# The attention of a decoder's second layer, moved from 49 single units to 33 steps of one or two, with its products in another order

## The chip, the cores and the metric

The kernel runs on one core of a Trainium2 chip. The metric is the device time of one execution in microseconds (us), taken as the median of several runs. The engines are named as in the profile: PE (TensorE, matrix products and transposes), PEld (its weight loads), DVE (VectorE), ACT (ScalarE), POOL (GpSimd) and SP (the queue that issues most DMAs).

## The reference

One inference step of a two-layer decoder for a prompt of 512 positions and 8 samples of 4 new positions each. Layer 1 is a Mamba-2 mixer; then one shared K/V is computed; layer 2 is attention in three dilation groups over that K/V, which the change is about. All arithmetic is in f32.

```python
D_MODEL, SEQ, DEC_BATCH, DEC_SEQ, PAST_LEN = 1024, 512, 8, 4, 1024
ATT_HEAD_DIM = 128; KV_HEADS = 8
WINDOWS, DILATIONS = (128, 512, 2048), (1, 4, 16)

def dilated_attn_prompt(q, k, v, bvec, dil, nw):      # and the same for samples, over the cached K/V
    scores = jnp.einsum("brnqhd,brnkhd->brnhqk", qs, kb) * (dh ** -0.5)
    scores = jnp.where(valid[None, None], scores + bias, NEG_INF)
    lse = jax.nn.logsumexp(scores, axis=-1)
    p = jnp.exp(scores - lse[..., None])
    o = jnp.einsum("brnhqk,brnkhd->brnqhd", p, vb)
    ...
def dilated_mixer(h, attend, biases, g_norm, w_in, w_out):
    u = rmsnorm(h, g_norm) @ w_in
    q, gate = ...                                     # 3 x 8 heads of queries, and a gate per head
    for g in range(N_DIL_GROUPS):
        o, lse = attend(q[:, :, g], biases[g], DILATIONS[g], WINDOWS[g] // DILATIONS[g])
    w = jax.nn.softmax(jnp.stack(lses, axis=0), axis=0)
    o = jnp.sum(w[..., None] * jnp.stack(outs, axis=0), axis=0)
    y = o.reshape(b, l, ATT_WIDTH) * jax.nn.silu(gate)
    return y.astype(h.dtype) @ w_out
```

## The kernel before, in words

The program is written in Python; a scheduler sets each engine's order from it, close to the order of writing. Each engine then works through its own queue in order and waits at an instruction whose inputs or buffers are not ready. Blocks marked `tc.high_priority()` are put earlier.

Layer 2 interleaves two streams on PE. The first is the *filler*: the projections of queries and gate, in products of 12 matmuls each (`product`, three for each of four blocks of the inner dimension, 128x272 results, tiles `pa` and `pb`). One filler matmul is called F. Seven products make a pair of heads' tiles, from sums and differences of weights (`sums`, L1266 to L1272). `cast(b + 3)` splits the weights of the product three ahead in a high part `whi` (ACT, L1289) and a low part `wlo` (DVE, L1290), into one of four buffers, which product b - 1 frees with its last matmul. Evacuations of the products are L1218 to L1244 (`qp`, `kv`, `us`, `y`; `u2`, `u3` appear as sums) and L1327 to L1333. `run(n)` issues the next n F. After the projections the filler goes on with the out projection, which needs the gated `y` split in high and low part (`yh` L1345, `yl` L1346).

The second stream is the attention, in *units*, each a generator that stops at `yield`:

- `attend(h, n)`, 32 times: head h, 128 queries of the prompt. Scores `sp` are one full product and eight (for the dilated groups) on 32 of the array's columns, "tiled" below; then on DVE two reduces (L1392, L1395) and the maximum (L1397), on ACT the exponential (L1398), on DVE an add of two groups and a reciprocal (L1399, L1400). Stop. Transposes `ptp` of the weights, copied on ACT to `pt`, `ptz`. Stop. The products with the values, `pv`, full ones and then tiled ones; `on` on ACT (L1419). Stop. Transpose `op`; a head's fourth goes to `y`.
- `sample(h, q)`, 16 times: four samples of head h. Cached keys `kc` come by DMA; scores `s` are tiled; softmax on DVE and ACT (L1460 to L1465). Stop. Transposes `w`. Stop. Products `so` with cached values, all tiled.
- `combine`, once: weights of the groups for all samples. Ln, `lse` (L1492), transpose `lp`, a softmax over groups (L1498 to L1516). Stop. Transpose `lp2`. Stop. Products `oc`.

The order is set by the list `units` and the loop at the end of the layer: pass u lets three older units go on by one stop (u - 4, then u - 2, then u - 3), starts unit u, and issues 24 F (20 from unit 44 on). `LA = 2` is the distance from a unit's start to its second part.

Of the kernel before, what the change touches and what calls it, by code (L numbers as in the profile page):

```python
# [34 lines left out]
ATH = 8  # L35
# [19 lines left out]
OCN, SKIP = 2, 1  # L55
POOL_A = (0, 1, 2, 3)
POOL_B = (0, 1, 2)
PRO, OFF, PACE = 9, 8, (57, 62, 64, 44)
LA, FILL, SLOW = 2, (24, 20), 44
TH = T // 2  # L60


# [65 lines left out]
def tile_yoco_step(  # L128
# [16 lines left out]
    def mm(*a, **k):  # L145
        pin(nc.tensor.matmul(*a, **k))  # L146
# [767 lines left out]
    live = []  # L914
# [457 lines left out]
    def attend(h, n):  # L1372
        bt, qp = bt_t[h], [qp_t[h, g] for g in range(3)]
        kv = kv_t[h]
        kt = kv[:, 0, :]
        vb, vr = (kv[:, i, 0:SEQ].rearrange("p (n d) -> p n d", n=4) for i in (1, 2))
        kp = kt[:, NS:T]
        ktr = kp.rearrange("p (n r i) -> p r n i", n=4, r=4)
        bt12 = bt[:, 256:512].rearrange("p (a c) -> p a c", a=2)
        w = 32 * (n + 1)  # L1380
        g0 = 128 if n == 0 else 256
        sp = pss("sp")
        k0 = max(0, n - 1) * 128
        for g in range(2):
            for r in range(4):
                mm(sp[32 * r:32 * r + 32, g0 + w * g:g0 + w * g + w],
                   qp[1 + g][:, 128 * n + 32 * r:128 * n + 32 * r + 32], ktr[:, r, 0:n + 1, :], start=True, stop=True)
        mm(sp[:, 0:g0], qp[0][:, 128 * n:128 * n + 128], kp[:, k0:128 * n + 128], start=True, stop=True)
        s_ = wk.tile([128, 512], F32, name="s", bufs=3)
        mx = wk.tile([128, 4], F32, name="mx", bufs=4)  # L1390
        s12 = s_[:, g0:g0 + 2 * w].rearrange("p (a c) -> p a c", a=2)
        nc.vector.tensor_tensor_reduce(out=s12, in0=sp[:, g0:g0 + 2 * w].rearrange("p (a c) -> p a c", a=2),  # L1392
                                       in1=bt12[:, :, 128 - w:128], scale=1.0, scalar=-3e38,
                                       op0=ALU.add, op1=ALU.max, accum_out=mx[:, 1:2])
        nc.vector.tensor_tensor_reduce(out=s_[:, 0:g0], in0=sp[:, 0:g0], in1=bt[:, 256 - g0:256], scale=1.0,  # L1395
                                       scalar=-3e38, op0=ALU.add, op1=ALU.max, accum_out=mx[:, 0:1])
        nc.vector.tensor_scalar(mx[:, 2:3], mx[:, 0:1], mx[:, 1:2], -1.0, op0=ALU.max, op1=ALU.mult)  # L1397
        nc.scalar.activation(s_[:, 0:g0 + 2 * w], s_[:, 0:g0 + 2 * w], AF.Exp, bias=mx[:, 2:3], accum_out=mx[:, 3:4])  # L1398
        nc.vector.tensor_tensor(s12[:, 0, :], s12[:, 0, :], s12[:, 1, :], op=ALU.add)  # L1399
        nc.vector.reciprocal(mx[:, 3:4], mx[:, 3:4])  # L1400
        yield
        tp = pss("ptp", (128, 3, 128))
        nk = g0 // 128
        for i in range(nk):
            transpose(tp[:, i, :], s_[:, 128 * i:128 * i + 128], ident)
        transpose(tp[0:w, 2, :], s_[:, g0:g0 + w], ident)
        pt = wk.tile([128, 2, 128], F32, name="pt", bufs=2)
        nc.scalar.copy(pt[:, 0:nk, :], tp[:, 0:nk, :])
        nc.scalar.copy(ptz[n][0:w, :], tp[0:w, 2, :])
        yield  # L1410
        pv = pss("pv")[:, 0:128]
        for i in range(nk):
            b = n - nk + 1 + i
            mm(pv, pt[:, i, :], vb[:, b, :], start=i == 0, stop=False, skip_group_check=True)
        for r in range(4):
            mm(pv[32 * r:32 * r + 32, :], ptz[n][:, 32 * r:32 * r + 32], vr[:, r, :],
               start=False, stop=True, skip_group_check=True)
        on = wk.tile([128, 128], F32, name="on", bufs=1)
        nc.scalar.activation(on, pv, AF.Copy, scale=mx[:, 3:4])  # L1419
        yield  # L1420
        if h not in op_t:
            op_t[h] = pss("op")
        op = op_t[h]
        transpose(op[:, 128 * n:128 * n + 128], on, ident)
        op_n[h] = op_n.get(h, 0) + 1
        yt = y_t[h // 4][:, h % 4, :]
        if h == 7 and op_n[h] >= 3:
            c0, c1 = ((128, SEQ), (0, 128))[op_n[h] - 3]
            y7 = yt[:, NS + c0:NS + c1]
            assert len(gated) == 2  # L1430
            nc.vector.scalar_tensor_tensor(y7, op[:, c0:c1], 0.5, y7, op0=ALU.mult, op1=ALU.mult)
            y_split(h, NS + c0, NS + c1)
        elif h < 7 and op_n[h] == 4:
            nc.vector.tensor_copy(yt[:, NS:T], op)
            att_done.add(h)
# [5 lines left out]
    def sample(h, q):  # L1441
# [27 lines left out]
        for jp in range(2):  # L1469
            vc.append(wk.tile([128, 2, 5, 128], F32, name="vc", bufs=2))  # L1470
            dma(vc[jp], cv[h, q, :, 2 * jp:2 * jp + 2, :, :])
        yield
        dma(vn[0:TS], dap(vnd, h * 128 + 4 * q * TS * ATH * 128, [[ATH * 128, TS], [TS * ATH * 128, 4], [1, 128]]))
        w1, w2 = pss("w1", (128, 4, 128)), pss("w2", (128, 2, 128))
        for i in range(5):
# [2 lines left out]
        nc.scalar.copy(wt[:, 0:4, :], w1)  # L1478
        nc.scalar.copy(wt[:, 4, :], w2[:, 0, :])
        nc.scalar.copy(wt[0:TS, 5, :], w2[0:TS, 1, :])  # L1480
        yield
        so = pss("so")[:, 0:128]
        for i in range(6):
# [6 lines left out]
    def combine():  # L1490
        nc.scalar.activation(lsm, lsm, AF.Ln)
        nc.vector.tensor_tensor(lse, lsm, lse, op=ALU.subtract)  # L1492
        lp = pss("lp")
        transpose(lp[0:16, 0:128], lse, ident)
        ltr = qpad[0][0:16]
        lt = ltr[:, 0:4, :]
        with tc.high_priority():
            nc.vector.tensor_copy(lt.rearrange("p a b -> p (a b)"), lp[0:16, 0:128])  # L1498
        lv = lt[:, :, 0:12].rearrange("p j (g t) -> p j t g", t=TS)
        lgv = lt[:, :, 0:12].rearrange("p j (g t) -> p g j t", t=TS)  # L1500
        red = ltr[:, 4, :].rearrange("p (a j t) -> p a j t", a=2, t=TS)
        mxg, sm_ = red[:, 0], red[:, 1]

        def all_groups(a):
            return a[:, None, :, :].to_broadcast([16, 3, 4, TS])

        with tc.high_priority():
            nc.vector.tensor_reduce(out=mxg, in_=lv, axis=AX.X, op=ALU.max)
            for g in range(3):
                nc.vector.tensor_tensor(lgv[:, g], lgv[:, g], mxg, op=ALU.subtract)  # L1510
            nc.scalar.activation(lt[:, :, 0:12], lt[:, :, 0:12], AF.Exp)
            nc.vector.tensor_reduce(out=sm_, in_=lv, axis=AX.X, op=ALU.add)
            nc.vector.reciprocal(sm_, sm_)
            for g in range(3):
                nc.vector.tensor_tensor(lgv[:, g], lgv[:, g], sm_, op=ALU.mult)
            nc.vector.memset(lt[:, :, 12:32], 0.0)  # L1516
        yield
        lp2 = pss("lp2")
        transpose(lp2[:, 0:16], lt.rearrange("p a b -> p (a b)"), ident[0:16, 0:16])
        cmw = sbt[:, 0:272].rearrange("p (a b) -> p a b", b=16)  # L1520
        ws, cm = cmw[:, 16, :], cmw[:, 0:16, :]
        with tc.high_priority():
            nc.vector.tensor_copy(ws, lp2[:, 0:16])
            nc.vector.tensor_tensor(cm, sel[:, None, :].to_broadcast([128, 16, 16]), bc(ws, 16), op=ALU.mult)
        yield
        oc = pss("oc", (128, ATH, 2, 16))
        for h in range(ATH):
            for q in range(2):
                mm(oc[:, h, q, :], o_s[:, q, h, :], cm[:, 2 * h + q, :], start=True, stop=True)
                if q:  # L1530
                    run(OCN)
        nc.scalar.copy(y_s, oc.rearrange("p h q c -> p h (q c)"))
        sample_y()
# [102 lines left out]
    def run(n):  # L1636
        m = min(n, ahead[0]) if n > OCN else 0
        ahead[0] -= m
        for _ in range(n - m):
            if next(fill, 0) == 0:  # L1640
                return

    units = [(f, (h, i)) for h in range(ATH - 1) for f, i in
             ((attend, 0), (sample, 0), (attend, 1), (attend, 2), (sample, 1), (attend, 3))]
    units += [(sample, (7, 0)), (attend, (7, 1)), (attend, (7, 2)), (sample, (7, 1)), (attend, (7, 3)), (combine, ()), (attend, (7, 0))]
    fill = filler()
    fetch_kv(0)
    for _ in range(2 * 84):
        next(fill)
    fetch_kv(1)  # L1650
    live = []
    for u in range(len(units) + LA + 2):
        i = u - LA
        if u == len(units) - 2 + SKIP:
            ahead[0] = ATH * OCN
        for j in (i - 2, i, i - 1):
            if 0 <= j < len(units):
                next(live[j], 0)
        if u < len(units):
            f, a = units[u]  # L1660
            if f is attend and a[0] not in bt_t:
                bt_t[a[0]] = bias_tile(a[0])
            if f is attend and a[1] == 2 and 0 < a[0] < ATH - 1:
                fetch_kv(a[0] + 1)
            live.append(f(*a))
            next(live[u])
        run(FILL[u >= SLOW])
    run(10000)
    bctx.close()

# [94 lines left out]
```

## Time and profile before

| | |
|---|---|
| Runs | 928.69, 927.66, 925.65 us; median 927.66 |
| Profiled execution | 932.11 us, its span 930.2 us |
| Granted clock of PE, mean | 0.996 |
| Busy over the span | PE 908.9, PEld 847.9, DVE 687.5, ACT 489.9, POOL 163.0 us |
| Attention stretch, 593.30 to 875.00 us | PE busy for 279.24 of 281.70 us |

The profiled execution is longer than the median of the runs. Rows of the profile name an engine, the line of the helper or program that issued the instruction, and the tiles: all matrix products stand under L146 and all transposes under L149, so they are told apart by tile (`sp`, `s`, `pv`, `so` and so on), with the pair `128*128` or `128*32` for a full or a tiled product. A bracket at a row's end is the time that the engine had been idle, and what released it.

### The profile page before, as it was taken

The page shows a single profiled execution, that of the slowest core. Times are in us where ns is not written, and L with a number is a line of the kernel's source. Part 1 is how long each engine was busy: PE and PEld are TensorE (multiplying, and loading weights), DVE is VectorE, ACT ScalarE, POOL GpSimd, SP SyncE. Part 2 cuts the span into 40 slices and gives each one's busy share as a digit, 9 for nine tenths or more (in the row PEclk, how much of TensorE's full clock was granted, in tenths as well). Part 3 has the DMA queues.
Part 4 walks back from the last instruction along what each step waited for, and adds up shares of the span by engine and source line. Part 5 has one row for each costly group of instructions (what it writes and reads, how often), then busy time and mean ns, then how long its engine had stood idle before and what let it go on. Part 6 is the DMA issues. An engine that isn't in the chain of part 4 may idle for free.

```text
span 930.2 us, 21888 instructions
## 1 busy us (share of the span) xinstructions
PE 908.9 (98%) x8671; PEld 847.9 (91%) x8671; DVE 687.5 (74%) x1435; ACT 489.9 (53%) x1140; POOL 163.0 (18%) x212
## 2 busy tenths in 40 slices
PE   8999999999999999999999999999999999999997
PEld 7989888888989889999999999999899999989997
DVE  6998899989799899644489335876677766778732
ACT  6678655655566655422255213555455555557642
POOL 2031344433514642111101001000000000000021
PEclk9999999999999999999999999999999999999999
DMA  8224365355364442536277556757768868774511
GB/s 295 93 74 155 104 206 166 121 170 170 134 201 161 149 165 101 156 108 228 90 256 227 183 184 196 265 182 264 252 203 262 280 204 267 270 256 155 194 49 49
DMA packets 80573, 168.48 MB, mean 181 GB/s; under 512 B 19990, under 2 KB 37736, under 8 KB 79960
## 3 DMA queue, kind: packets, MB, share of 16 engines
q1 hardware_dynamic: 73784, 154.60, 50.5%
q10 hardware_dynamic: 5616, 9.75, 2.8%
q0 software_dynamic: 1072, 2.74, 1.1%
q8 instruction: 68, 1.11, 0.5%
q14 instruction: 33, 0.27, 0.1%
HBM read 141.14 MB, written 25.93 MB: 180 GB/s over the span
## 4 chain that ended last, share of the span: by engine, by line
PE 82%; DVE 9%; DMA 4%; ACT 2%; issue 2%; POOL 0%; SPq 0%; POOLq 0%; DVEq 0%; ACTq 0%
PE pa L146 33%; PE pb L146 28%; PE sp L146 3%; PE pv L146 2%; PE so L146 2%; PE s L146 2%; DVE wlo L206 2%; DMA kc<-ck 1%; PE yd L146 1%; DMA m<-aed 1%; DVE co L641 1%; PE csp L146 1%; PE w L149 1%; PE ptp L149 1%; PE xp L149 1%
## 5 line engine op out<-in xcount | busy, mean ns | idle before, releaser
L205 ACT ACTIVATE whi<-wraw 128x1024 fp32r<-128x1024 f32 x69 | 72.8, 1056 | 97.0 <-PE pb L146 57.2
L206 DVE TENSOR_TENSOR wlo<-wraw,whi 128x1024 fp32r<-128x1024 f32 x69 | 89.6, 1298 | 45.1 <-ACT whi L205 44.7
L146 PE MATMUL pa<-bq,whi 128*128 128x272 f32 x512 | 103.1, 296 | 0.0
L146 PE MATMUL pb<-nl,whi 128*128 128x288 f32 x280 | 84.0, 300 | 0.0
L146 PE MATMUL pb<-nh,wlo 128*128 128x288 f32 x280 | 83.5, 298 | 0.0
L146 PE MATMUL pb<-nh,whi 128*128 128x288 f32 x280 | 83.4, 298 | 0.0
L146 PEld LDWEIGHTS pa<-bq,whi 128*128 128x128 f32 x512 | 81.2, 189 | 0.9
L146 PE MATMUL pa<-nh,whi 128*128 128x256 f32 x280 | 81.1, 290 | 0.5 <-DVE uz L681 0.5
L146 PE MATMUL pa<-nl,whi 128*128 128x256 f32 x280 | 80.7, 288 | 0.0
L146 PE MATMUL pa<-nh,wlo 128*128 128x256 f32 x280 | 80.1, 286 | 0.0
L146 PE MATMUL pb<-bq,whi 128*128 128x272 f32 x384 | 77.2, 296 | 1.3 <-DVE kv L1230 1.1
L146 PE MATMUL pa<-bq,wlo 128*128 128x272 f32 x256 | 74.2, 290 | 0.0
L641 DVE SCALAR_TENSOR_TENSOR co<-cb,cvp,co 128x568 f32<-128x568 f32 x72 | 64.0, 892 | 1.5 <-ACT co L639 0.9
L146 PEld LDWEIGHTS pb<-bq,whi 128*128 128x128 f32 x384 | 60.8, 189 | 2.6 <-DVE kv L1230 1.3
L1289 ACT ACTIVATE whi<-wraw 128x512 fp32r<-128x512 f32 x64 | 40.1, 627 | 35.2 <-PE pb L146 16.8
L146 PEld LDWEIGHTS pb<-nl,whi 128*128 128x128 f32 x280 | 53.0, 189 | 4.4 <-issue 4.4
L146 PEld LDWEIGHTS pa<-nh,whi 128*128 128x128 f32 x280 | 53.8, 192 | 2.6 <-issue 1.9
L146 PE MATMUL pb<-bq,wlo 128*128 128x272 f32 x192 | 55.5, 289 | 0.0
L146 PEld LDWEIGHTS pa<-nl,whi 128*128 128x128 f32 x280 | 53.8, 192 | 1.4 <-issue 1.4
L146 PEld LDWEIGHTS pb<-nh,wlo 128*128 128x128 f32 x280 | 53.1, 190 | 2.2 <-issue 2.2
L146 PEld LDWEIGHTS pa<-nh,wlo 128*128 128x128 f32 x280 | 53.8, 192 | 0.9 <-issue 0.9
L146 PEld LDWEIGHTS pb<-nh,whi 128*128 128x128 f32 x280 | 53.0, 189 | 0.8 <-issue 0.8
(408 smaller groups left out, 2788.0 us busy)
## 6 DMA issues: line engine op xcount, KB each, us to landing
wraw<-w_in SPq DMA_DIRECT2D x40, 512.0 KB
kc<-ck SPq DMA_DIRECT2D x32, 640.0 KB
vc<-cv SPq DMA_DIRECT2D x32, 640.0 KB
wraw<-wb SPq DMA_DIRECT2D x32, 512.0 KB
s<-s SPq DMA_DIRECT2D x32, 256.0 KB
m<-aed SPq DMA_DIRECT2D x16, 512.0 KB
ssmS<-s ACTq DMA_DIRECT2D x32, 256.0 KB
wraw<-w_out SPq DMA_DIRECT2D x16, 512.0 KB
```

The costliest lines, as they stand in the source:

```text
L146: pin(nc.tensor.matmul(*a, **k))
L149: pin(nc.tensor.transpose(*a))
L205: a = nc.scalar.activation(hi, raw, AF.Copy)
L206: b = lo_eng.tensor_tensor(lo, raw, f32(hi), op=ALU.subtract)
L641: nc.vector.scalar_tensor_tensor(o, cb[:, k:k + n], cvp[:, ti, k:k + 1], o, op0=ALU.mult, op1=ALU.add)
L1289: nc.scalar.activation(hi, src[p][j], AF.Copy)
```

## The change

Units are joined in 33 steps: for each head, sample 0 with block 0, block 1, sample 1 with block 2, block 3 (the last head has its block 0 after `combine`). `LA` is 1: a unit's transposes come one step after its scores. In a pass, the step three back goes on first, then the one before, then the one two back, twice; within a step the prompt's unit goes ahead of the sample's. New stops cut `sp` (tiled | full) and `pv` (full | tiled) so that tiled products of several units follow on each other. Each pass issues 36 F, the last three scored steps 40, 24 and 40, and 20 after that. The lines of the program behind `attend`'s scores move by one to six.

```diff
-LA, FILL, SLOW = 2, (24, 20), 44
+LA = 1
...
                    qp[1 + g][:, 128 * n + 32 * r:128 * n + 32 * r + 32], ktr[:, r, 0:n + 1, :], start=True, stop=True)
+        yield
         mm(sp[:, 0:g0], qp[0][:, 128 * n:128 * n + 128], kp[:, k0:128 * n + 128], start=True, stop=True)
...
             mm(pv, pt[:, i, :], vb[:, b, :], start=i == 0, stop=False, skip_group_check=True)
+        yield
         for r in range(4):
...
-    units = [(f, (h, i)) for h in range(ATH - 1) for f, i in
-             ((attend, 0), (sample, 0), (attend, 1), (attend, 2), (sample, 1), (attend, 3))]
-    units += [(sample, (7, 0)), (attend, (7, 1)), (attend, (7, 2)), (sample, (7, 1)), (attend, (7, 3)), (combine, ()), (attend, (7, 0))]
+    steps = [[(f, (h, i)) for f, i in st] for h in range(ATH - 1) for st in
+             (((sample, 0), (attend, 0)), ((attend, 1),), ((sample, 1), (attend, 2)), ((attend, 3),))]
+    steps += [[(sample, (7, 0)), (attend, (7, 1))], [(attend, (7, 2))], [(sample, (7, 1)), (attend, (7, 3))],
+              [(combine, ())], [(attend, (7, 0))]]
+    fills = [36] * (4 * (ATH - 1)) + [40, 24, 40]
...
-        for j in (i - 2, i, i - 1):
-            if 0 <= j < len(units):
-                next(live[j], 0)
+        for j in (u - LA - 2, u - LA, u - LA - 1, u - LA - 1):
+            if 0 <= j < len(steps):
+                for g_ in live[j][::-1]:
+                    next(g_, 0)
...
+            live.append([f(*a) for f, a in steps[u]])
+            for _ in range(2):
+                for g_ in live[u]:
+                    next(g_, 0)
-        run(FILL[u >= SLOW])
+        run(fills[u] if u < len(fills) else 20)
```

(`sample` has a second `yield` at each of its two stops, and `combine` at its two, to go with the passes.)

The order shows at three places what this moves. Names are as above; `bq` is the filler's input.

**PE, where head 0's block 1 is transposed.** Before:

```order
L149 MATMUL op<-ident,on 128x128
L149 MATMUL ptp<-ident,s 128x128 x2
L149 MATMUL ptp<-ident,s 64x128
L146 MATMUL so<-vc,wt 32x128 x20
L146 MATMUL so<-vn,wt 32x128 x4
L146 MATMUL s_7624<-kc,qpad_7031 32x512 x4
L146 MATMUL s_7625<-kc,qpad_7031 32x128 x4
L146 MATMUL s_7625<-kv,qpad_7031 32x4 x4
L146 MATMUL pb<-bq_6915,whi 128x272 x2
```

And now:

```order
L149 MATMUL ptp<-ident,s 128x128 x2
L149 MATMUL ptp<-ident,s 64x128
L146 MATMUL pv<-kv,pt 128x128
L146 MATMUL pv<-kv,ptz_7035 32x128 x4
L146 MATMUL so<-vc,wt 32x128 x20
L146 MATMUL so<-vn,wt 32x128 x4
L146 MATMUL s_7569<-kc,qpad_7031 32x512 x4
L146 MATMUL s_7570<-kc,qpad_7031 32x128 x4
L146 MATMUL s_7570<-kv,qpad_7031 32x4 x4
L146 MATMUL sp<-kv,qp 32x96 x8
L146 MATMUL sp<-kv,qp 128x256
```

The samples' tiled products stood between a transpose and F in a block of their own; they now lie between the tiled part of `pv` and that of `sp`.

**DVE, around the maximum and the add of head 6's block 2** (`ISA` rows are the reduces; the number behind waits only says for which engine's semaphore). Before:

```order
L1392 ISA s,mx<-sp,bt 128x192 [waits PE_49]
L1392 ISA mx 128x1
L1395 ISA s,mx<-sp,bt 128x256
L1395 ISA mx 128x1
L1397 TENSOR_SCALAR mx<-mx 128x1 [waits DVE_49]
L1329 SCALAR_TENSOR_TENSOR sums<-pb,sums 128x272 [waits PE_49,Activation_49]
L1399 TENSOR_TENSOR s<-s 128x96 [waits Activation_49]
```

And now:

```order
L1290 TENSOR_TENSOR wlo<-sums,whi 128x512 [waits PE_49,Activation_49]
L1237 SCALAR_TENSOR_TENSOR kv<-kv,pa 128x240 [waits Activation_49]
L1272 TENSOR_TENSOR sums<-wraw,sums 128x512 [waits DVE_49]
L1333 SCALAR_TENSOR_TENSOR sums<-pa,sums 128x272 [waits PE_49]
L1290 TENSOR_TENSOR wlo<-wraw,whi 128x512 [waits Activation_49]
L1239 SCALAR_TENSOR_TENSOR us<-kv,pa 128x32
L1244 SCALAR_TENSOR_TENSOR y_7023<-y_7023,kv 128x240 [waits DVE_49]
L1398 TENSOR_SCALAR mx<-mx 128x1
L1400 TENSOR_TENSOR s<-s 128x96 [waits Activation_49]
```

The maximum followed on the reduces; now two casts and the evacuations of two products stand between.

**PE, in the tail, from combine's second transpose on** (`lp_11373` and `lp_11321` are the tile `lp2`). Before, with the transposes of block 3 well ahead of it:

```order
L149 MATMUL op<-ident,on 128x128
L149 MATMUL ptp<-ident,s 128x128 x3
L146 MATMUL so<-vc,wt 32x128 x20
L146 MATMUL so<-vn,wt 32x128 x4
L146 MATMUL sp<-kv,qp 32x32 x8
L146 MATMUL sp<-kv,qp 128x128
L146 MATMUL pa<-bq_6917,wlo 128x272
L146 MATMUL pa<-bq_6917,whi 128x272 x2
L146 MATMUL pa<-bq_6917,wlo 128x272
L149 MATMUL lp_11373<-ident,qpad_7031 128x16
L146 MATMUL pv<-kv,pt 128x128 x2
L146 MATMUL pv<-kv,ptz_7038 32x128 x4
```

And now:

```order
L149 MATMUL lp_11321<-ident,qpad_7031 128x16
L146 MATMUL pv<-kv,pt 128x128 x2
L146 MATMUL pv<-kv,ptz_7038 32x128 x4
L146 MATMUL so<-vc,wt 32x128 x20
L146 MATMUL so<-vn,wt 32x128 x4
L146 MATMUL sp<-kv,qp 32x32 x8
L146 MATMUL sp<-kv,qp 128x128
L146 MATMUL pa<-bq_6917,whi 128x272
L146 MATMUL pa<-bq_6917,wlo 128x272
L146 MATMUL pa<-bq_6917,whi 128x272 x2
L149 MATMUL op<-ident,on 128x128
L149 MATMUL ptp<-ident,s 128x128
```

`lp2` comes ahead of the last samples' products, and the last unit's transposes come after four F and an `op`, where 24 F stood before.

More of the change, by code (lines that the diff above doesn't have):

```diff
@@ L1472, in sample @@
         yield
+        yield
         dma(vn[0:TS], dap(vnd, h * 128 + 4 * q * TS * ATH * 128, [[ATH * 128, TS], [TS * ATH * 128, 4], [1, 128]]))
@@ L1480, in sample @@
         nc.scalar.copy(wt[0:TS, 5, :], w2[0:TS, 1, :])
+        yield
         yield
@@ L1517, in combine @@
         yield
+        yield
         lp2 = pss("lp2")
@@ L1524, in combine @@
             nc.vector.tensor_tensor(cm, sel[:, None, :].to_broadcast([128, 16, 16]), bc(ws, 16), op=ALU.mult)
+        yield
         yield
@@ L1651, in tile_yoco_step @@
     live = []
-    for u in range(len(units) + LA + 2):
-        i = u - LA
-        if u == len(units) - 2 + SKIP:
+    for u in range(len(steps) + LA + 2):
+        if u == len(steps) - 2 + SKIP:
             ahead[0] = ATH * OCN
-        for j in (i - 2, i, i - 1):
-            if 0 <= j < len(units):
-                next(live[j], 0)
[L1659 to L1666, printed above, removed]
-        run(FILL[u >= SLOW])
+        for j in (u - LA - 2, u - LA, u - LA - 1, u - LA - 1):
+            if 0 <= j < len(steps):
+                for g_ in live[j][::-1]:
+                    next(g_, 0)
+        if u < len(steps):
+            for f, a in steps[u]:
+                if f is attend and a[0] not in bt_t:
+                    bt_t[a[0]] = bias_tile(a[0])
+                if f is attend and a[1] == 2 and 0 < a[0] < ATH - 1:
+                    fetch_kv(a[0] + 1)
+            live.append([f(*a) for f, a in steps[u]])
[3 more added lines that the diff above has]
+        run(fills[u] if u < len(fills) else 20)
     run(10000)
```

## The prediction

> **What bounds the kernel now.** I read the page's engine and chain lines first, then one window over the attention stretch, then TensorE's waits there, then the timeline at the places where the change puts something else.
>
> ```profile
> PE 908.9 (98%) x8671; PEld 847.9 (91%) x8671; DVE 687.5 (74%) x1435; ACT 489.9 (53%) x1140; POOL 163.0 (18%) x212
> PE 82%; DVE 9%; DMA 4%; ACT 2%; issue 2%; POOL 0%; SPq 0%; POOLq 0%; DVEq 0%; ACTq 0%
> ```
>
> TensorE (PE) is busy for 98% of the span and carries 82% of the chain that ended last. The attention stretch, from the first prompt scores to the end of the attention's products (start us:end us, length, then busy time of PE, weight loads, DVE, ACT, POOL, the granted clock, DMA share, GB/s):
>
> ```profile
> 593.30:875.00 281.70, 279.24 (x3566) 254.16 (x3566) 204.55 (x631) 161.19 (x429) 4.59 (x16) 1.00 0.72 239
> ```
> ```profile
> PE s L146 <- DMA kc<-ck: 1.4, 3, 0.6
> PE pb L146 <- DVE kv L1230: 1.1, 1, 1.1
> ```
>
> PE idles for 2.5 us of 281.7, and its waits of any size are four: three for the cached keys and one for an evacuation at the end. So there are two ways to gain here, cheaper switches between kinds of product and those 2.5 us, and every new wait of PE is a loss in full. No wait for a softmax stands in the list.
>
> **Switches between tiled and full products.** Rows of PE's timeline (start, duration, instruction; 128*128 marks a full product, 128*32 a tiled one):
>
> ```profile
> 678.83 0.27 PE L149 MATMUL op<-ident,on 128*128 128x128 f32 x1
> 678.93 0.49 PE L149 MATMUL ptp<-ident,s 128*128 128x128 f32 x3
> 679.36 1.30 PE L146 MATMUL so<-vc,wt 128*32 128x128 f32 x40
> ...
> 681.77 0.22 PE L146 MATMUL s<-kv,qpad 128*32 128x4 f32 x8
> 681.92 0.52 PE L146 MATMUL pb<-bq,whi 128*128 128x272 f32 x2
> 682.28 0.29 PE L146 MATMUL pb<-bq,wlo 128*128 128x272 f32 x1
> ...
> 683.53 0.41 PE L146 MATMUL pa<-bq,whi 128*128 128x272 f32 x2
> ...
> 685.03 0.49 PE L149 MATMUL ptp<-ident,s 128*128 128x128 f32 x3
> 685.36 0.61 PE L146 MATMUL pv<-kv,pt 128*128 128x128 f32 x4
> ```
>
> Twelve filler products (F from here) run from 683.53 to 685.03, 0.125 us each. Three transposes with a full product behind them take 0.33 (685.03 to 685.36), and with a tiled one behind them 0.43 (678.93 to 679.36): going into tiles costs 0.10. Going out: from the last tiled scores at 681.77 to F at 681.92 is 0.15, and the first two F take 0.36 (681.92 to 682.28) instead of 0.25. Of both I count 0.19 as the price of the way out, since the scores themselves need some of the 0.15. Counted in the order of PE, the stretch has 50 blocks of tiled products before and 33 now: samples' so and s, the prompt's pv tail and the tiled part of sp follow on each other. Sixteen times an entry and an exit go (the seventeenth block is in the tail): 16 x (0.10 + 0.19) = 4.6 us gained, on PE and so on the path. Bounds: 16 x 0.19 = 3.0 if only the way out is saved, 16 x (0.10 + 0.15 + 0.11) = 5.8 if all of it is. I take 4.6, as the two measured spots say. The rule in the Trainium skill (TensorEngine Tiling (Array Packing), section Key Properties) is that a change of tiling mode drains the array; the rows agree as to kind, with 0.10 and 0.19 us.
>
> **What the nearer transposes run into.** A unit's scores and the transposes of its softmax weights lay two passes apart, 2 x 24 F = 6.0 us; now one step, 36 F = 4.5 us. The chain between them is two reduces and a maximum on DVE, the exponential on ACT, an add on DVE. Where little stands in its way it is short, as a late unit shows (head 7's block 0, the last: its scores, what DVE and ACT did, a wait of PE that has another cause, and its transposes):
>
> ```profile
> 856.63 0.73 PE L146 MATMUL sp<-kv,qp 128*32 128x32 f32 x18
> ...
> 857.70 0.39 DVE L1237 SCALAR_TENSOR_TENSOR kv<-kv,pa 128x240 f32<-128x240 f32 x1
> ...
> 858.02 0.17 DVE L1239 SCALAR_TENSOR_TENSOR us<-kv,pa 128x32 f32<-128x32 f32 x1
> 858.12 0.41 DVE L1244 SCALAR_TENSOR_TENSOR y<-y,kv 128x240 f32<-128x240 f32 x1
> ...
> 859.76 0.28 DVE L1395 CUSTOM_DVE_ANT_0 s<-sp,bt 128x128 f32<-128x128 f32 x1
> ...
> 860.30 0.21 DVE L1397 TENSOR_SCALAR mx<-mx 128x1 f32<-128x1 f32 x1
> ...
> 860.54 0.46 ACT L1398 ACTIVATE s<-s,mx 128x192 f32<-128x192 f32 x1 [1.03 <-DVE mx L1397]
> ...
> 861.12 0.19 DVE L1399 TENSOR_TENSOR s<-s 128x32 f32<-128x32 f32 x1 [0.61 <-ACT s L1398]
> ...
> 861.78 0.52 PE L146 MATMUL pb<-bq,whi 128*128 128x272 f32 x2 [1.06 <-DVE kv L1230]
> ...
> 863.00 0.38 PE L149 MATMUL ptp<-ident,s 128*128 128x128 f32 x2
> ```
>
> From the start of the maximum to the end of the add are 1.0 us (860.30 to 861.31); two reduces, of 0.28 as the one at 859.76 or somewhat more, and the hand-offs from PE and back make it about 2 us. But DVE and ACT work in the order of their queues, and what stands ahead may wait for PE itself. The casts of the filler's weights (whi on ACT, wlo on DVE) write to buffers that a product of 12 F frees with its last. The same spot a little earlier shows an add that stood behind such a pair:
>
> ```profile
> 851.93 0.19 ACT L1398 ACTIVATION_READ_ACCUMULATOR s<-s,mx 128x1 f32 x1
> ...
> 852.67 0.69 DVE L1290 TENSOR_TENSOR wlo<-sums,whi 128x512 fp32r<-128x512 f32 x1 [1.28 <-ACT whi L1289]
> ...
> 853.27 0.28 DVE L1399 TENSOR_TENSOR s<-s 128x128 f32<-128x128 f32 x1
> ```
>
> The exponential ended at 852.12, and the add began at 853.27: 1.15 us, as DVE came first to the cast wlo, which had waited 1.28 for its whi. It cost nothing there, since PE had the rest of 48 F to do. With 36 F the stretch holds three casts, freed by its 12th, 24th and 36th F. I went through the orders of ACT and DVE against PE's: in 4 of the 28 steps of heads 0 to 6, the exponential or the add stands behind the cast that only the stretch's last F frees; before, none stood behind one that its own last stretch freed so late. The wait of PE then is the last F's 0.29, the cast 0.63, and either the exponential (0.62 of 128x384, and 0.12 to its add) or wlo (0.60 to the next), the add 0.22, hand-offs 0.05, less what PE still does meanwhile (its F 0.125, op 0.10):
>
> ```profile
> L1289 ACT ACTIVATE whi<-wraw 128x512 fp32r<-128x512 f32 x52 | 32.5, 626 | 18.6 <-PE pa L146 9.8 <-PE pb L146 5.5 <-ACT whi L1289 2.5
> L1398 ACT ACTIVATE s<-s,mx 128x384 f32<-128x384 f32 x8 | 4.9, 616 | 8.6 <-DVE mx L1397 8.6
> L1399 DVE TENSOR_TENSOR s<-s 128x64 f32<-128x64 f32 x8 | 1.7, 218 | 1.6 <-ACT s L1398 1.6
> ```
>
> That is 1.6 us, three times 4.8. In the fourth, head 6's block 2, the maximum itself stands behind wlo, us and y: 0.29 + 0.63 + 0.60, us and y 0.10 + 0.41, the maximum 0.24, exponential and add 0.74 + 0.22, less 0.23: 3.0. Three more steps end with DVE behind by about half a microsecond, 1.4. Together +9. Ends: 0, if these casts are ready when the softmax comes, and 12, if each of the four waits for one more wlo of 0.69.
>
> **The tail** (the last head's blocks, combine, the start of the out projection), rows of the timeline of before:
>
> ```profile
> 849.14 0.17 DVE L1492 TENSOR_TENSOR lse<-lsm,lse 128x16 f32<-128x16 f32 x1 [0.18 <-ACT lsm L1491]
> ...
> 849.36 0.75 DVE L1346 TENSOR_TENSOR yl<-y,yh 128x240 fp32r<-128x240 f32 x2
> ...
> 850.48 0.27 PE L149 MATMUL op<-ident,on 128*128 128x128 f32 x1
> ...
> 852.14 0.28 PE L149 MATMUL lp<-ident,lse 128*16 128x128 f32 x1
> ...
> 855.28 0.20 DVE L1512 TENSOR_REDUCE qpad<-qpad 16x16 f32<-16x48 f32 x1
> ...
> 855.67 0.37 ACT L1232 ACTIVATE kv<-pa 128x272 f32<-128x272 f32 x1
> 855.72 0.23 DVE L1513 RECIPROCAL qpad<-qpad 16x16 f32<-16x16 f32 x1
> ...
> 856.77 0.33 DVE L1515 TENSOR_TENSOR qpad<-qpad 16x16 f32<-16x16 f32 x3
> ...
> 857.79 0.23 PE L149 MATMUL lp<-ident,qpad 16*128 16x16 f32 x1
> ```
>
> - lse, the input of combine's first transpose lp, stood ahead of the splits yl in DVE's order and was ready 2.8 us early (849.31 to 852.14). Now there stand between the scores of block 3 and lse: eight yl at 0.37 (half of the pair's 0.75), three wlo at 0.60, six evacuations and gatings of some 0.1 to 0.4 (2.0), and the unit's own reduces, maximum, add and two reciprocals (1.5): 8.3 us, and 0.5 for hand-offs and lse itself. PE does 40 F in that time and the 1.66 from op to lp (850.48 to 852.14): 6.7. So lp waits 2.1 (0 to 4, by how far ACT keeps up with its side of these splits).
> - From lp to lp2, combine's second transpose, were 5.65 us. Now PE has 20 F and an op there, 2.6 us. The exponential on the way stands on ACT behind an evacuation of a product that ends with the 16th of the 20 F: 2.0 + 0.29, the evacuation 0.37, then on DVE kv, us and y (0.75 from start to next), and the rest of combine 0.20 + 0.23 + 0.33 with hand-offs of 0.4: 4.6. So lp2 waits 2.0 (0.9, if the evacuation's gating doesn't come between, to 3.0).
> - The last unit, head 7's block 0: scores to transposes were 856.63 to 863.00 with 24 F; now 4 F and an op are between. Its chain of 2.0 to 2.2 less 0.6: +1.5 (1.0 to 1.7). The F that waited 1.06 for kv waits again, less by 0.5, as its chain is less crowded.
> - The first block of the out projection waits for the last block's gating, which now ends after that chain: +1.0 (0 to 1.5).
>
> Tail: 2.1 + 2.0 + 1.5 - 0.5 + 1.0 = +6. PE's moved order leaves the DMA queue of SP nearly as it was: a head's first sample comes ahead of its first prompt unit, and cached keys are asked for one step of 36 F and a block ahead, about as far as before; the 1.4 us in the waits may come back or go: 0 (-1.4 to +1.4). Instructions, weight fetches and casts are the same in number.
>
> **Sum**: -4.6 + 9 + 6 = +10.4, rounded to +10; with all lower ends -5.8 + 0 + 1, with all upper ends -3.0 + 12 + 9. On the profiled execution (932.11 us, 4.4 above the median shown) it would be 942; on the median 927.66 it gives 937.5.
>
> **Rivals.**
> - Queues with slack: whatever stands ahead of exponential, add and lse is done when PE arrives. For it: ACT is busy for 57% and DVE for 73% of the stretch, and no softmax wait is in the list of before. Against: the order puts work that PE frees last ahead of them. It decides whether the add ends before the 36th F. Then -4.6 - 0.5 is left: 922.5, faster.
> - Stalls hidden in the 28 steps, tail as worked out: -4.6 + 6, 929, no change.
> - Half of the stalls (the casts come one product earlier in two of the four): -4.6 + 4.5 + 5, 932.5.
> - Switches save nothing, as weight loads hide them: +15, 942.5.
> - The clock. In the stretch it is granted at 1.00, with a longest wait of PE of 1.06 us. A wait of 3 us, as in head 6, is longer than any there; should the clock halve for one stretch of 36 F, that adds 36 x 0.125 = 4.5 us: 942. The Trainium skill (TensorE: Matmul & The Clock Gate, section Why this matters for your kernels) says that a gap of about 3 us between bursts brings the slow clock back; no run here shows it, and the row of 1.06 at a full clock is no case of it.
>
> **Numbers.** Forecast 0.60 (934 to 942), half of the stalls 0.14, slack 0.10, steps hidden but not the tail 0.07, clock 0.05, switches 0.04. The runs before spread over 925.65 to 928.69, so 0.3% (2.8 us) is about what can be told from no change: faster 0.10, same 0.07, slower 0.83. The range of 930 to 944 leaves out the slack case and most of the 929.
>
> **What would show it.** PE's waits should list ptp (transposes) behind DVE's add or ACT, in a few steps, 1.5 us each and once about 3, and lp, lp2 and the last ptp behind DVE in the tail; PE's busy time in the stretch should fall by 4 to 5 us while the stretch grows by 10. If ptp waits less than 3 us in all, or PE's busy time doesn't fall, the step concerned is wrong.

## The result and the profile after

The changed kernel took 943.62 us in the median of six runs (939.59 to 946.96) against 927.94 for the kernel before (six runs, 925.65 to 929.06): a ratio of 1.0168, 95% interval 1.0141 to 1.0195. It is slower by 15.7 us where 9.8 were forecast.

The profiled execution took 942.79 us with a span of 941.0, 10.8 longer than that of before. In it layer 1, whose code is the same, was 3.7 us shorter: the filler's first F started at 568.0 and not at 571.7. From that first F to the end it is 373.0 against 358.5, so 14.5 us were lost in the part that the change touches, close to the difference of the medians. The page's engine line, the counterpart of the one shown of before:

```profile
PE 908.7 (97%) x8671; PEld 848.3 (90%) x8671; DVE 686.9 (73%) x1435; ACT 491.1 (52%) x1140; POOL 160.4 (17%) x212
```

No engine has more to do. One window from the filler's first F to the out projection's first (start:end, length, busy time of PE, weight loads, DVE, ACT, POOL, granted clock, DMA share, GB/s), of before and then of after:

```profile
571.70:868.79 297.09, 294.43 (x3681) 269.31 (x3680) 218.75 (x652) 168.14 (x441) 7.18 (x26) 1.00 0.73 241
```
```profile
568.00:878.41 310.41, 295.28 (x3692) 270.83 (x3691) 217.37 (x651) 168.97 (x440) 5.95 (x26) 0.99 0.69 229
```

The window grew by 13.3 us. PE's idle time in it grew from 2.7 to 15.1 us, its busy time by 0.85, and the mean clock fell below 1.00. (Of the busy time, 0.7 us are the last block's products with the values, which stood behind the out projection's first product before, outside this window.) The idle time is what PE's waits in the same window list (in all, times, longest):

```profile
PE ptp L149 <- ACT s L1399: 6.4, 5, 3.0
PE ptp L149 <- DVE s L1400: 3.5, 4, 1.2
PE lp L149 <- DVE qpad L1519: 2.3, 1, 2.3
PE lp L149 <- DVE lse L1496: 1.4, 1, 1.4
PE pb L146 <- DVE qp L1221: 0.9, 2, 0.7
PE pb L146 <- DVE kv L1230: 0.5, 1, 0.5
```

PE now waits for the softmax nine times; before it never did. The waits for cached keys are gone. Two of the places, in the order of time. The first is head 0's block 1, where ACT casts weights that PE frees late and the exponential stands behind:

```profile
602.79 0.29 PE L146 MATMUL pa<-bq,wlo 128*128 128x272 f32 x1
602.88 0.21 DVE L1398 TENSOR_SCALAR mx<-mx 128x1 f32<-128x1 f32 x1
603.05 0.63 ACT L1289 ACTIVATE whi<-wraw 128x512 fp32r<-128x512 f32 x1 [0.89 <-PE pa L146]
...
603.58 0.60 ACT L1399 ACTIVATE s<-s,mx 128x384 f32<-128x384 f32 x1
...
604.33 0.56 PE L149 MATMUL ptp<-ident,s 128*128 128x128 f32 x3 [1.25 <-ACT s L1399]
```

The cast began at 603.05, when the stretch's last F was over; ACT had been idle for 0.89 before it. The maximum was there at 603.09, and the exponential began at 603.58. The second is head 6's block 2, which the prediction worked out by itself; here the maximum stands behind a cast, us and y on DVE:

```profile
816.89 0.27 PE L149 MATMUL op<-ident,on 128*128 128x128 f32 x1
817.02 0.63 ACT L1289 ACTIVATE whi<-wraw 128x512 fp32r<-128x512 f32 x1 [0.58 <-ACT kv L1232]
...
817.72 0.44 DVE L1333 SCALAR_TENSOR_TENSOR sums<-pa,sums 128x272 f32<-128x272 f32 x1
818.07 0.69 DVE L1290 TENSOR_TENSOR wlo<-wraw,whi 128x512 fp32r<-128x512 f32 x1
818.67 0.18 DVE L1239 SCALAR_TENSOR_TENSOR us<-kv,pa 128x32 f32<-128x32 f32 x1
818.76 0.41 DVE L1244 SCALAR_TENSOR_TENSOR y<-y,kv 128x240 f32<-128x240 f32 x1
...
819.08 0.21 DVE L1398 TENSOR_SCALAR mx<-mx 128x1 f32<-128x1 f32 x1
...
819.33 0.67 ACT L1399 ACTIVATE s<-s,mx 128x448 f32<-128x448 f32 x1 [1.68 <-DVE mx L1398]
...
820.14 0.60 PE L149 MATMUL ptp<-ident,s 128*128 128x128 f32 x3 [2.98 <-ACT s L1399]
```

And the clock. Three windows of 6 us, the only ones in the stretch in which it was under 1.00:

```profile
736.00:742.00 6.00, 3.98 (x47) 3.17 (x49) 4.85 (x13) 2.24 (x7) 0.00 (x0) 0.79 0.63 229
742.00:748.00 6.00, 6.00 (x96) 5.12 (x89) 3.08 (x16) 2.54 (x6) 0.18 (x1) 0.92 0.63 216
820.00:826.00 6.00, 5.86 (x50) 4.90 (x51) 1.32 (x7) 2.00 (x8) 0.00 (x0) 0.72 0.65 194
```

The third follows the wait of 2.98 us; the first two follow two waits of 1.16 and 0.86 us at 738 and 740. The work lost is 6 x (0.21 + 0.08 + 0.28) = 3.4 us.

### The profile page after: what moved, and what is told of

Same layout as the page of the kernel before. It is cut to its first block, busy times and chain, and to the rows that moved or that the text cites. A ratio compares the mean times of both kernels' runs of the same rounds, so it can differ in the third digit from the quotient of the medians.

```text
span 941.0 us, 21900 instructions
## 1 busy us (share of the span) xinstructions
PE 908.7 (97%) x8671; PEld 848.3 (90%) x8671; DVE 686.9 (73%) x1435; ACT 491.1 (52%) x1140; POOL 160.4 (17%) x212
```

## The experiments

Two theories stood against each other. **Queue theory**: the softmax stands behind casts that PE frees last, at a distance of only 36 F, and the waits (with the clock) cost more than the fewer switches save. **Order theory**: the joined order of products is itself slower on PE, and the waits are by-products. The windows named here run from the filler's first F to the out projection's, as above.

### Two steps of distance, and where the values are fetched

```diff
-LA = 1
+LA = 2
```

> The changed kernel with a distance of two steps (72 F) instead of one from scores to transposes; the order of the products within a step stays. Queue theory (the softmax stands behind casts that PE frees last): the waits of ptp in the 28 steps fall from 9.1 us to under 1, and so do both stretches at half clock (3.4 us); if the cached keys come in time the run is at 930 to 934. The keys' transfers now stand behind those of the values, which wait two steps longer for their buffer, so waits of s for kc of up to 2 us per sample may take the place, and the time stays near 944. Order theory (the joined order of products is itself slower): ptp may fall, but PE's busy time in the stretch stays at or above 295 us and the time above 938 without any wait for kc.

Measured: 943.12 us, 1.0158 of before (1.0135 to 1.018). ptp is no longer in the list of waits at all, and this stands at its top:

```profile
PE s L146 <- DMA kc<-ck: 11.7, 13, 1.8
```

One wait was exchanged for another, and by the time alone nothing would have been seen. The clock dipped once in the stretch, from about 660, behind two such waits of 1.54 and 0.45 us; two of 1.55 and 0.45 at 622 to 624 left it alone. On SP's queue the keys of a sample stand behind the values of the one before, and these wait for a buffer that `so` frees (15 times, 60.0 us in all), now a step later. The second run takes the values off that queue:

```diff
-LA = 1
+LA = 2
...
-            dma(vc[jp], cv[h, q, :, 2 * jp:2 * jp + 2, :, :])
+            nc.gpsimd.dma_start(vc[jp], cv[h, q, :, 2 * jp:2 * jp + 2, :, :])
```

> As the one with two steps, but the cached values are fetched from POOL's DMA queue instead of SP's, so that keys don't stand behind them. Queue theory: no waits for ptp in the steps, waits for kc under 2 us in all, the clock at 1.00 throughout, and the gain of fewer switches becomes visible: PE's busy time in the stretch 3 to 5 us under before's 294.4; 922 to 926 us, faster than before. Order theory: not under 930.

Measured: 924.16 us, 0.9957 of before (0.9942 to 0.9973), the first version that is faster. Its window, and all of PE's waits in it:

```profile
567.20:859.80 292.60, 288.41 (x3682) 266.92 (x3681) 218.21 (x652) 167.77 (x441) 22.69 (x58) 1.00 0.75 244
```
```profile
PE lp L149 <- DVE lse L1496: 1.5, 1, 1.5
PE pa L146 <- ACT sums L1327: 1.3, 1, 1.3
PE pb L146 <- DVE qp L1221: 0.5, 1, 0.5
PE pb L146 <- DVE kv L1230: 0.5, 1, 0.5
PE s L146 <- ACT ptz L1410: 0.2, 1, 0.2
```

Without waits of ptp and at a full clock, PE's busy time is 288.4 us, 6.0 less than before's 294.4, where 3 to 5 were expected. That speaks against the order theory. Two reservations: the samples' `s` and `so` now lie in different steps, though the blocks of tiled products are about as few (35 in PE's timeline, 34 in the changed kernel, 51 before); and not all of the 6.0 is the gain of the switches. Before's busy time also holds scores that late keys drew out: one head, from 644.17 to 679.36, took 35.19 us against 32.88 of an undisturbed one, 2.3 more, of which only 1.05 are listed as waits. The switches alone are read from undisturbed heads below.

### The two controls for POOL's queue

The same edit of the values' queue alone, on the changed kernel with one step and on the kernel before.

> The changed kernel at its distance of one step, only the cached values fetched from POOL's DMA queue: the control for the two-step version with that queue. If the distance from scores to transposes is what counts, ptp still waits for 5 to 10 us in the 28 steps and the time is 937 to 943. If the queue of the values made the gain, the time falls to about 925.

> The kernel before, only the cached values fetched from POOL's DMA queue. If the gain of the two-step version comes from fewer switches, this one loses no more than the 1.4 us of waits for kc: 926 to 928. If the queue made it, 924.

Measured: 945.42 us (1.0195 of before, 1.0161 to 1.0229) with one step, and 929.12 (1.0015, 0.9998 to 1.0032; 926 to 928 were expected) on the kernel before. With one step the waits of ptp stayed:

```profile
PE ptp L149 <- DVE s L1400: 4.8, 4, 1.7
PE ptp L149 <- ACT s L1399: 4.2, 5, 2.0
```

```profile
568.30:885.00 316.70, 301.31 (x3692) 276.51 (x3690) 217.95 (x651) 167.84 (x441) 22.40 (x58) 0.96 0.69 227
```

The time came out above what was expected, and the mean clock in the window is 0.96, the lowest of all versions: 0.04 x 316.7 = 12.7 us of work lost, by rounding 11 to 14, in five dips. The profile is that of the run of 950.02 us, whose mean clock was 0.982; the fastest of the six, 941.86 us, had 0.992. So the queue alone gains nothing, in either kernel. Distance alone gained nothing either (the first run). Both together do.

### Casts at plain priority

```diff
-            with tc.high_priority():
-                nc.scalar.activation(hi, src[p][j], AF.Copy)
-                nc.vector.tensor_tensor(lo, src[p][j], f32(hi), op=ALU.subtract)
+            nc.scalar.activation(hi, src[p][j], AF.Copy)
+            nc.vector.tensor_tensor(lo, src[p][j], f32(hi), op=ALU.subtract)
```

> The changed kernel, its casts of the filler's weights issued without raised priority, so that they stand in the order of writing, mostly behind the softmax of the step. Queue theory: waits of ptp in the 28 steps fall from 9.1 to about 3 us, the half-clock stretch after the 3.0 us wait goes, the tail's 4.8 us stay: 934 to 938 us. Order theory: no change, 941 to 946.

Measured: 937.55 us, 1.0101 (1.0081 to 1.0121), 6 us less than the changed kernel. The window fell from 310.4 to 303.2 us:

```profile
570.50:873.70 303.20, 293.32 (x3692) 269.52 (x3691) 216.12 (x651) 168.73 (x440) 5.94 (x26) 1.00 0.72 235
```
```profile
PE ptp L149 <- ACT s L1398: 2.8, 3, 1.0
PE ptp L149 <- DVE s L1399: 2.7, 3, 1.3
```

Products, transposes and their order on PE are the same as in the changed kernel; only where the casts stand on ACT and DVE differs. The waits of ptp fell from 9.9 to 5.5 us (with 0.8 in the tail in both, so to 4.7 in the 28 steps, where about 3 were expected), and there was no dip of the clock in the stretch. This is the direct evidence for the casts; the 5.5 that are left show that they are not all of it.

### Blocks of tiled products cut in two

On the kernel before, four of a pass's 24 F are run between a sample's values of one unit and the scores of the next.

```diff
+        n_ = FILL[u >= SLOW]
+        if u < len(units) and units[u][0] is sample:
+            run(4)
+            n_ -= 4
         if u < len(units):
...
-        run(FILL[u >= SLOW])
+        run(n_)
```

> The kernel before, with four of the 24 F moved to between a sample's values of one unit and the scores of the next, so that each of 16 blocks of tiled products is cut in two. If a switch into and out of tiled products costs 0.29 us, PE's busy time grows by 4.6 us and the time by 4 to 5, besides 0 to 3 in the tail, where combine's transpose moves nearer to its softmax: 932 to 935. If weight loads hide the switches: 928, but for the tail.

Measured: 939.34 us, 1.0125 (1.0105 to 1.0145), more than expected. The window, its only stretch with a lower clock, and the largest wait:

```profile
569.80:875.10 305.30, 301.17 (x3682) 271.08 (x3681) 221.35 (x652) 167.89 (x441) 6.39 (x26) 0.99 0.71 234
857.00:863.00 6.00, 5.57 (x57) 5.25 (x61) 4.02 (x20) 2.00 (x6) 0.00 (x0) 0.72 0.42 136
```
```profile
PE lp L149 <- DVE lse L1492: 3.1, 1, 3.1
```

PE's busy time grew by 6.7 us, of which the dip is 6 x 0.28 = 1.7; 5.0 are left. PE's timeline has 66 blocks of tiled products here and 51 before, so 15 blocks were cut and not 16: ahead of the first sample's scores there are only F. That is 0.33 for each, where two spots of the trace had given 0.29. An undisturbed head shows it without dip or wait. From one sample's `so` to that of the same sample of the next head, 144 F in all, in the kernel before, with the cuts, and in the changed kernel:

```profile
679.36:712.24 32.88, 32.88 (x434) 30.04 (x433) 23.94 (x72) 17.96 (x49) 0.37 (x2) 1.00 0.78 245
677.33:710.92 33.59, 33.59 (x435) 30.05 (x434) 24.39 (x73) 17.97 (x49) 0.37 (x2) 1.00 0.76 250
639.13:671.46 32.33, 32.33 (x441) 29.96 (x436) 20.83 (x67) 17.91 (x50) 0.37 (x2) 1.00 0.81 268
```

Two cuts in a head cost 0.71 us. Two blocks fewer in a head save 0.55 us in the changed kernel itself (0.59 with two steps and POOL's queue, and with the casts at plain priority, where such heads take 32.29), so 4.4 to 4.7 us over eight heads. The joined order is the faster one, which speaks most directly against the order theory.

In the tail, combine's first transpose waits 3.1 us, the upper end of what was expected there, and the dip behind it was not expected. With these, 5.0 + 3.1 + 1.7 = 9.8 of the 11.5 us between the medians are accounted for.

### One wait in an undisturbed stretch

On the kernel before, five copies in place on DVE between the add and the transposes of one unit; they add work and change no value.

```diff
         nc.vector.reciprocal(mx[:, 3:4], mx[:, 3:4])
+        if (h, n) == (4, 1):
+            for _ in range(5):
+                nc.vector.tensor_copy(s_[:, 0:g0 + 2 * w], s_[:, 0:g0 + 2 * w])
         yield
```

> The kernel before, with five copies in place more on DVE between the add and the transposes of head 4's block 1: one wait of PE of about 3.6 us in a stretch that had none. If a wait of 3 us or more brings the half clock, the window behind it shows 0.50 for about 3 us and the work behind loses 1.7 us beside the wait; if the dips in the changed kernel had another cause (many waits, load of the other engines), the clock stays at 1.00.

Measured in one run: 931.94 us. The wait was shorter than expected, and the clock fell all the same:

```profile
PE ptp L149 <- DVE s L1403: 2.3, 1, 2.3
```
```profile
742.00:748.00 6.00, 5.75 (x83) 4.57 (x84) 2.27 (x7) 1.22 (x5) 0.00 (x0) 0.72 0.45 131
```

The transposes started at 742.25. A single wait of 2.3 us cost another 6 x 0.28 = 1.7 us of work behind it. But in the changed kernel the wait of 2.30 us ahead of lp2, with one of 1.36 five microseconds earlier, left the clock alone:

```profile
856.00:862.00 6.00, 3.77 (x35) 3.16 (x33) 5.44 (x19) 4.86 (x14) 0.00 (x0) 1.00 0.15 27
862.00:868.00 6.00, 3.81 (x85) 3.40 (x85) 3.44 (x19) 1.89 (x6) 0.00 (x0) 1.00 0.63 248
```

The version with one step and POOL's queue has the same pair of waits in its tail, 1.37 and 2.30 us, and there the clock did fall. It also fell there behind a wait of 1.71 us at 780:

```profile
780.00:786.00 6.00, 6.00 (x104) 4.72 (x105) 3.01 (x9) 1.27 (x5) 1.05 (x2) 0.72 0.88 247
864.00:870.00 6.00, 5.26 (x85) 4.83 (x85) 2.14 (x11) 1.28 (x4) 0.00 (x0) 0.72 0.51 206
```

So the length of a wait alone does not decide; what does is open.

### The tail

Fillers were moved between the last steps, in two versions: with the casts at plain priority and one step, and with two steps and POOL's queue.

```diff
-    fills = [36] * (4 * (ATH - 1)) + [40, 24, 40]
+    fills = [36] * (4 * (ATH - 1)) + [36, 24, 48, 36, 24]
```

> The version at one step with the casts at plain priority, and fillers moved in the tail: the last steps get 36, 24, 48, 36 and 24 F instead of 40, 24, 40, 20 and 20. If the tail's waits are a matter of too few F between lse, combine's two transposes and the last unit, lp and lp2 (1.4 us each) no longer wait, and the time falls by 3 to 5 us, to 933 to 935; what is left over the kernel before are the waits of ptp in the steps (about 4.5 us), with their half clock, and one for an evacuation in the tail, less the gain of the switches. If the tail's work is late for other reasons, the waits only move: 936 to 938.

Measured: 937.18 us in the median (1.0081, 1.0051 to 1.0111), not told apart from the 937.55 without it, and inside the 936 to 938 that were expected if the waits only move; its runs go from 929.81 to 938.02. In the profiled one lp and lp2 no longer wait, as expected, but PE waits for a cast instead, and nine microseconds later the clock is low for about 10 us:

```profile
PE pb L146 <- DVE wlo L1289: 2.0, 1, 2.0
```
```profile
864.00:876.00 12.00, 12.00 (x63) 12.00 (x63) 4.79 (x11) 2.98 (x7) 0.00 (x0) 0.57 0.30 89
```

That is 12 x 0.43 = 5.2 us of lost work. What brought the clock down there is not shown. The run of 929.81 us was not profiled, but its mean clock is on record: 0.999, against 0.988 to 0.992 in the five others. From these, an estimate: 0.007 to 0.011 of some 935 us, 7 to 10 us less work lost, and it was 7.4 us under the median. So the two waits went, and the slow clock hides in the median what that is worth; how much the tail costs by itself this version does not show.

> The two-step version with POOL's queue, and fillers moved in the tail: the last steps get 24, 24, 48, 36 and 36 F instead of 40, 24, 40, 20 and 20, so that 48 F lie ahead of combine's first transpose and 36 on either side of its second. The waits left in the tail there are 1.5 us for lse and 1.3 us for an evacuation: if they go, 922 to 923; if the late work only meets another wait, 924 to 925.

Measured: 923.19 us, 0.9944 (0.9925 to 0.9963), against 924.16 without the moved fillers: the wait for lse went, and the two versions can't be told apart by time.

## Why the prediction was right, and by how much it was off

The direction and the mechanism came out; the sum of +10 was 5.7 short of the measured 15.7. The median of 943.62 lies above the 934 to 942 that had most of the chance and 0.4 us inside the range's end of 944, which three of the six runs exceeded: that the range held is in part luck.

- **Waits in the 28 steps, +9.** Measured 9.1 us: 1.25, 1.16, 0.33, 1.16 + 0.86, 1.12, 0.28 and 2.98. The 3.0 worked out for head 6's block 2 is the row of 2.98, along the forecast chain but for two links: the cast wlo came 0.4 us later, behind an evacuation (L1333), and the transposes did not wait for the add (0.22). Where three waits of 1.6 were forecast there are four places, three of 1.1 to 1.25, as the first transposes need only the exponential and not the add, which the prediction counted in, and one of 2.0 in two parts; and of the three small ones there are two, 0.33 and 0.28. That the sum agrees so well is in part luck. The cause was right (the casts): at plain priority the waits fell by 4.4 us. What the 4.7 that stayed stood behind was not told apart; with two steps they went too.
- **Tail, +6.** Measured 4.8 on the waits: lp 1.4 (2.1 forecast), lp2 2.3 (2.0), the last ptp 0.8 (1.5), kv -0.5 (-0.5), and in the out projection a wait of 0.7 for a weight cast and 0.2 for yl (1.0, but the forecast had only the last block's gating in mind, to which the 0.2 belongs).
- **Switches, -4.6.** PE's busy time in the window did not fall by 4 to 5 us but rose by 0.85, and by the prediction's own sign this step would be wrong. The sign was ill chosen: that busy time also holds the slow clock (3.4), the last block's products (0.7), and matmuls drawn out by late keys. Heads without any of these show the switches alone: 0.55 us saved in each, 4.4 over eight. The cuts, the other way, cost 0.33 us each.
- **The clock, taken as a rival at 0.05, with 4.5 us.** This is the step that failed: it was not an alternative to the forecast but came on top of it, in two places, with 3.4 us. The row behind the rival was right, the wait of 3 us; its chance was mis-sized, and two waits of about 1 us in a row did it too. Its price was too high, 4.5 us for one stretch where each dip cost 1.7. The rule of the Trainium skill (TensorE: Matmul & The Clock Gate, section Why this matters for your kernels), that gaps above about 3 us bring back the slow clock, agrees as to kind, but its length is too long here: 2.27 us was enough once, 1.71 once, and 1.16 + 0.86.
- **Keys, 0.** The listed waits went, -1.4; what late keys cost beyond the list was not measured for either kernel as a whole.
- **Smaller:** waits for the evacuation qp, +0.7, not forecast. Each wait is counted short by about 0.17, as behind an op, since that row lasts 0.27 us and the next product would start 0.10 after it; over ten such waits that is 1.7 us, an estimate. It belongs to the busy time.

Together: 9.1 + 4.8 + 3.4 - 1.4 + 0.7 + 1.7 - 4.4 = 13.9, of the 14.5 us between first F and end; 0.6 stays unassigned. The rest of the distance to the 15.7 of the medians lies between executions.

Of the rivals, slack in the queues, hidden stalls and half of the stalls are out (nine waits of ptp, 9.1 us in the steps), and so are switches that save nothing (the undisturbed heads, and the cuts).

## What to carry to other kernels

Where an engine without slack takes its work from queues in order, the distance between a producer and its consumer has to cover the last thing that stands ahead of the producer in its queue, and here that was work that the busy engine itself frees at the end of the same stretch; look for it in the order of the queues, not in the share of busy time. A gain in the order of products showed in the run's time only once the distance was doubled and the queue that the doubling blocked was emptied, and each of the two edits alone showed nothing; in the trace it could be read all along, from one head without wait or dip. Price a new wait with the clock behind it: 1.7 us more here, behind some waits of 1.5 to 3 us and not behind others.

## What the runs showed of the hardware

- The granted clock fell to one half after waits of PE of 1.71, 2.27, 2.98 and 3.1 us, and after 1.16 + 0.86 within 3 us. A dip mostly cost 1.7 us of work, which at half the clock is 3.4 us, and in two executions (one step with the values on POOL's queue, and one step with fillers moved in the tail) one lasted about 10.
- The same waits did not always do it: after 2.30 us ahead of lp2 it fell in one execution and not in another, and after 1.54 + 0.45 us but not after 1.55 + 0.45 in the same one.
- A block of tiled products among full ones cost 0.33 us in switches (5.0 us over 15 cuts), with the entry at 0.10 in the rows; taking two such blocks out of a head saved 0.55 us.
